# Query, key and value columns of the first attention layer as seven block products per group, in a stage of their own

## The chip, the cores and the metric

The kernel runs on one core of a Trainium2 chip. The metric is the device time of one execution in microseconds (us), the median of several executions. The core's engines are TensorE (PE in the profile, with its weight loads as PEld), VectorE (DVE), ScalarE (ACT), GpSimd (POOL) and SyncE (SP). SP and ACT also issue the DMAs: a row "SPq" or "ACTq" is such an issue.

## The reference

The reference is a trunk of two layers on 1024 tokens of width 1024. Each layer normalizes its input, multiplies it by one wide matrix, runs a token mixer and a cross attention into 256 memory tokens, multiplies by a gate and adds an output projection to the input. Only the first layer's mixer is of interest here:

```
cols = h @ w_in_a                                # 1024 tokens x 1024 -> 9216 columns for the mixer
qkv = cols.reshape(B, S, 3, N_GROUPS, A_HEADS, HEAD_DIM)
q = rms_norm(qkv[:, :, 0], q_gain); k = rms_norm(qkv[:, :, 1], k_gain); v = qkv[:, :, 2]
q = apply_partial_rotary(q, cos, sin); k = apply_partial_rotary(k, cos, sin)
for g, (window, dil) in enumerate(((128, 1), (512, 4), (2048, 16))):
    o, lse = dilated_window_attention(q[:, :, g], k[:, :, g], v[:, :, g], dil, window // dil)
alpha = softmax(stack(lses)); o = sum(alpha * outs)      # per head, over the three groups
```

So there are nine column blocks of 1024 x 1024 (query, key and value for three groups g = 0, 1, 2 with dilations 1, 4 and 16), each of eight heads of 128 columns. A query of a group sees at most 129 keys, its own and those before it at steps of the dilation.

## The kernel before

**Precision.** Each float32 operand of a projection is split in two, a rounded part and the remainder ("hi" and "lo"; for weights `wh` and `wl`), and three matmuls per 128 rows of depth (hi x hi, hi x lo, lo x hi) stand for one exact product. `piece` (L195 issues the load) brings a 128x1024 piece of weights from DRAM into `raw`; ACT rounds it to `wh` (L166, the line of the copy helper) and DVE forms `wl` (L212). `project` (L252 to L254) is the inner loop: a tile of 128 tokens stands still in PE, 512 weight columns stream past it, 24 matmuls for a tile and a block of 512 columns.

**Stages.** From 0 to about 70 us the input is normalized and transposed into `hhi` and `hlo`, and the first half of the gate's columns is projected. To about 245 us the memory's keys and values and the memory queries follow, with the cross attention and four slices of its gate (`gate_mem`). To 1250 us six rounds run, one for each half Q of the heads and each group g, from dilation 16 to dilation 1. A round projects keys, values and queries of four heads (`project_tiles`, eight token tiles each) and keeps keys and values in SBUF. After it come the second half of the gate and the output projection (to about 1420 us), then the second layer (to the end), which the change leaves alone.

**Within a round.** A key or query tile goes through `head_norm`: ACT squares it (`sq`, L300), DVE sums (L302), POOL raises to the power -1/2 (`rsqrt`, L175), DVE scales it out of PSUM (`qn`, L305). POOL then rotates it (`rotary`, L894 to L898), PE transposes four heads (`heads_T`, L311), and ACT copies them out (keys L1003, queries L166). As soon as a query tile is there, `attend` runs for the tile before it: scores (L954 to L957), mask and row maximum on DVE (L963), exponential on ACT (L965), transposes (L970), copy to SBUF on DVE (L972), values (L976). Its instructions stand among the next query tile's matmuls in PE's queue. Groups 1 and 2 write their outputs and row statistics to DRAM (`o_scr`, `st_scr`); group 0 reads them back and merges the three (`merge`; ACT scales one at L926, DVE adds the others at L929).

**Order of the tokens.** The token tiles are kept in the order by residue that the group in hand needs; before dilation 4 and before dilation 1 the whole operand is copied into another order (`second_order`, `first_order`).

**What sets the order.** Every engine works through its own queue in program order, with semaphores between the engines; a scheduler puts the emitted instructions in queue order, mostly as they are written. Weights are taken from a plan (`ahead`, `take`): loads go out on SP's queue some pieces ahead. ACT also issues all DMAs that write to DRAM, in line with its computing.

## Time and profile before

| | |
|---|---|
| median of 3 runs | 2154.14 us (2151.47 to 2155.81) |
| span of the profiled execution | 2151.6 us |
| PE busy | 2131.4 us, 99% |
| DVE, ACT, POOL busy | 1059.3, 730.2, 370.5 us |
| the six rounds | 245 to 1250 us |
| DMA traffic | 183.49 MB |

The profiled execution's own time is its span, 2.5 us under the median of the runs. The rows of the profile are shown in the prediction. A row of groups reads: line, engine, operation, output<-inputs, partitions x elements, count; then the time busy and the mean duration of one in ns; then the idle time of that engine just ahead of them, and what ended it.

### The profile page before, as it was taken

How to read it: one execution, taken by the hardware profiler on the slowest of the kernel's cores; microseconds unless marked ns; L12 is line 12 of the kernel's file. 1: busy time of each engine (PE TensorE's matmuls, PEld its weight loads, DVE VectorE, ACT ScalarE, POOL GpSimd, SP SyncE). 2: the span in 40 equal slices, each digit the busy share in tenths (PEclk: the TensorE clock that was granted, in tenths of full speed). 3: DMA queues.
4: the chain of work that ended last, by engine and by line, in shares of the span. 5: the costliest groups of instructions: out<-in, count | busy, mean ns of one | idle time of the engine just before them, and what ended most of it. 6: DMA issues, size and time to landing. Idle time of an engine off the chain costs nothing. (4 is left out here: it accounts for less than half of the span.)

```text
span 2151.6 us, 29608 instructions
## 1 busy us (share of the span) xinstructions
PE 2131.4 (99%) x11273; PEld 1812.9 (84%) x11273; DVE 1059.3 (49%) x2403; ACT 730.2 (34%) x1507; POOL 370.5 (17%) x600
## 2 busy tenths in 40 slices
PE   8999999999999999999999999999999999999999
PEld 6888888888888888888888978888888888888887
DVE  6755323424414314425834755434557772776443
ACT  4545323323423323323422532233532221232211
POOL 1013212312313302312222100012200000000221
PEclk9999999999999999999999999999999999999999
DMA  6543211221221121111411375431301112112633
GB/s 201 135 145 65 54 41 53 65 59 43 57 70 50 49 59 50 50 49 55 117 57 51 117 249 180 129 97 44 103 22 56 57 55 59 50 57 91 235 121 114
DMA packets 181004, 183.49 MB, mean 85 GB/s; under 512 B 49008, under 2 KB 117760, under 8 KB 180864
## 3 DMA queue, kind: packets, MB, share of 16 engines
q1 hardware_dynamic: 116592, 138.48, 21.1%
q10 hardware_dynamic: 64272, 43.13, 7.1%
q8 instruction: 89, 1.46, 0.3%
q14 instruction: 51, 0.42, 0.1%
HBM read 138.45 MB, written 43.12 MB: 84 GB/s over the span
## 5 line engine op out<-in xcount | busy, mean ns | idle before, releaser
L254 PE MATMUL acc<-wh,hlo 128*128 128x512 f32 x1440 | 565.3, 394 | 0.0
L253 PE MATMUL acc<-wl,hhi 128*128 128x512 f32 x1440 | 565.2, 393 | 0.0
L252 PE MATMUL acc<-wh,hhi 128*128 128x512 f32 x1440 | 563.1, 394 | 1.4 <-ACT wh L166 1.1
L175 POOL TENSOR_TENSOR rr<-rv,nhalf 128x4 f32<-128x4 f32 (+1 forms) x150 | 147.4, 983 | 1372.2 <-DVE rv L173 1346.5
L212 DVE TENSOR_TENSOR wl<-raw,wh 128x1024 fp32r<-128x1024 f32 x152 | 187.9, 1238 | 377.4 <-ACT wh L166 375.7
L252 PEld LDWEIGHTS acc<-wh,hhi 128*128 128x128 f32 x1440 | 271.1, 188 | 55.2 <-ACT wh L166 1.5
L253 PEld LDWEIGHTS acc<-wl,hhi 128*128 128x128 f32 x1440 | 270.9, 188 | 53.4 <-DVE wl L212 0.4
L254 PEld LDWEIGHTS acc<-wh,hlo 128*128 128x128 f32 x1440 | 270.7, 188 | 53.2
L166 ACT ACTIVATE wh<-raw 128x1024 fp32r<-128x1024 f32 x152 | 160.7, 1058 | 189.7 <-PE acc L254 55.2
L540 PE MATMUL acc<-hhi,wl 128*128 128x512 f32 x512 | 203.8, 398 | 0.0
L539 PE MATMUL acc<-hlo,wh 128*128 128x512 f32 x512 | 203.6, 398 | 0.0
L538 PE MATMUL acc<-hhi,wh 128*128 128x512 f32 x512 | 202.9, 396 | 0.0
L302 DVE TENSOR_REDUCE ss<-sq 128x4 f32<-128x512 f32 x116 | 79.2, 683 | 144.3 <-ACT sq L300 144.1
L635 PE MATMUL acc<-wh,yhi 128*128 128x512 f32 x360 | 143.2, 400 | 3.2 <-ACT yhi L166 3.2
L636 PE MATMUL acc<-wl,yhi 128*128 128x512 f32 x360 | 141.6, 393 | 0.0
L637 PE MATMUL acc<-wh,ylo 128*128 128x512 f32 x360 | 140.5, 395 | 0.0
L300 ACT ACTIVATE sq<-acc 128x512 f32<-128x512 f32 x116 | 68.9, 594 | 181.2 <-PE acc L254 177.1
L305 DVE TENSOR_TENSOR qn<-acc,rr 128x512 f32<-128x512 f32 x116 | 79.6, 688 | 93.5 <-PE pt L311 50.6
L965 ACT ACTIVATE pa<-pa,st 128x128 f32<-128x128 f32 (+1 forms) x192 | 84.4, 442 | 99.5 <-DVE st L963 95.4
L539 PEld LDWEIGHTS acc<-hlo,wh 128*128 128x128 f32 x512 | 96.3, 188 | 17.9
L538 PEld LDWEIGHTS acc<-hhi,wh 128*128 128x128 f32 x512 | 96.3, 188 | 17.6
L540 PEld LDWEIGHTS acc<-hhi,wl 128*128 128x128 f32 x512 | 96.3, 188 | 17.6
(241 smaller groups left out, 3193.3 us busy)
## 6 DMA issues: line engine op xcount, KB each, us to landing
raw<-in_w_in_a_dram SPq DMA_DIRECT2D x88, 512.0 KB
raw<-in_w_in_b_dram SPq DMA_DIRECT2D x40, 512.0 KB
o_scr<-os ACTq DMA_DIRECT2D x48, 256.0 KB
raw<-in_w_mem_kv_dram SPq DMA_DIRECT2D x16, 512.0 KB
os<-o_scr SPq DMA_DIRECT2D x32, 256.0 KB
raw<-in_w_out_a_dram SPq DMA_DIRECT2D x12, 512.0 KB
raw<-in_w_out_b_dram SPq DMA_DIRECT2D x12, 512.0 KB
gt<-gateb_scr SPq DMA_DIRECT2D x24, 256.0 KB
```

Source lines behind the costliest of these rows:

```text
L166: A.activation(dst, src, AF.Copy)
L175: G.tensor_tensor(r[:], v[:], nhalf[:, :n], op=OP.pow)
L212: rests.append(W_LO.tensor_tensor(lo[:], raw[:], hi[:].bitcast(F32), op=OP.subtract).ins)
L252: T.matmul(ps, hi, wh[:, j, :], start=at == 0, stop=False)
L253: T.matmul(ps, hi, wl[:, j, :], start=False, stop=False)
L254: T.matmul(ps, lo, wh[:, j, :], start=False, stop=at == n - 1)
L538: T.matmul(to, wh[:, k, :], mh, start=k == 0, stop=False)
L539: T.matmul(to, wh[:, k, :], ml, start=False, stop=False)
L540: T.matmul(to, wl[:, k, :], mh, start=False, stop=k == 7)
L635: T.matmul(pss[ch][:], hi[:, k, :], wh[:, j, :], start=first and k == 0, stop=False)
L636: T.matmul(pss[ch][:], hi[:, k, :], wl[:, j, :], start=False, stop=False)
L637: T.matmul(pss[ch][:], lo[:, k, :], wh[:, j, :], start=False, stop=end and k == 3)
```

## The change

For each of the nine column blocks, the matrix of 1024 tokens by 1024 rows of depth and the matrix of 1024 rows by 1024 columns are cut into four 512x512 blocks each. The ordinary product needs eight products of such blocks; the scheme of Strassen and Winograd needs seven, and sums of blocks ahead of and behind them.

- The tokens stay in natural order throughout. `x_pair` makes the operand two token tiles at a time (tile j and tile j+4) and with it the four sums s1 to s4 of input blocks, rounded on ACT, with remainders on POOL. s1 takes the place of a block (a21), which is kept in DRAM and read back during the last group.
- `load` brings the four weight blocks of a group from DRAM, `combine` forms their sums on POOL (eight passes of 128x1024 per group), `split_side` rounds them on ACT and forms the remainder on DVE, one product ahead.
- `product` runs a product: four token tiles of 12 matmuls. ACT copies the results of the first three products to SBUF; DVE adds later ones to these out of PSUM (four passes on POOL, L950 of the kernel after).
- `projected` does norm, rotary, transposes and the copy out, now from SBUF, and writes queries and keys to DRAM (`qk_scr`): one DMA per tile for group 0, four for groups 1 and 2, which put the tokens into residue order in runs of 32 tokens (128 bytes) or 16 tokens (64 bytes). Values go to `v_scr`.
- All nine groups are done first (keys, values, queries for g = 2, 1, 0), then the memory stage, then attention. Attention runs by pairs of heads: 12 pairs, eight tiles each, with queries, keys and values fetched two pairs ahead (`fetch`). Scores for two key blocks are one float32 product. The weighted sum of the groups is made by POOL (three passes for two tiles) and DVE (two).
- The memory gate's slices move: two stand in the memory stage, one is written ahead of attention, one between dilation 4 and dilation 1. The reordering copies and an extra pair of weight buffers go.

What stands in the queues now is shown at three places. First PE's queue at the first attention of dilation 16 (`s` scores, `pt` transposed probabilities, `po` output). Before it was:

```order
L254 MATMUL acc<-wh,hlo 128x512
L957 MATMUL s<-kT,qT 128x128
L970 MATMUL pt<-ident,pa 128x128 x2
L957 MATMUL s<-kT,qT 128x128
L970 MATMUL pt<-ident,pa 128x128 x2
L957 MATMUL s<-kT,qT 128x128 x2
L252 MATMUL acc<-wh,hhi 128x512
L253 MATMUL acc<-wl,hhi 128x512
L254 MATMUL acc<-wh,hlo 128x512
```

and after the change, behind the last product of the memory's cross attention (`po<-pml,vmh`):

```order
L398 MATMUL po<-pml,vmh_7779 128x256
L1078 MATMUL s<-kT,qT 128x128 x6
L1093 MATMUL pt<-ident,pa 128x128 x2
L1078 MATMUL s<-kT,qT 128x128 x2
L1093 MATMUL pt<-ident,pa 128x128 x2
L1078 MATMUL s<-kT,qT 128x128 x2
L1101 MATMUL acc<-vv,pts 128x128 x2
L1093 MATMUL pt<-ident,pa 128x128 x2
L1078 MATMUL s<-kT,qT 128x128 x2
```

The projection's matmuls that stood between the steps of attention are gone; the steps of two or three tiles alternate with one another.

Second ACT's queue where the keys of dilation 16 end and the values begin. Before, with `kT` the keys' place in SBUF and `vv` the values':

```order
L300 ACTIVATE sq<-acc 128x512 x2
L166 ACTIVATE wh<-raw 128x1024 x2
L1003 ACTIVATE kT<-pt,gqk 128x512 x2
L300 ACTIVATE sq<-acc 128x512
L166 ACTIVATE wh<-raw 128x1024 x2
L1003 ACTIVATE kT<-pt,gqk 128x512 x2
L166 ACTIVATE vv<-acc 128x512 x6
```

After, with `os` the transposed heads and `x_` the first results of the next group:

```order
L910 ACTIVATE os<-pt,gqk 128x4x16x8
L154 ACTIVATE x_1706<-acc 128x512
L918 DMA qk_scr_97<-os 128x8x16 x4
L910 ACTIVATE os<-pt,gqk 128x4x16x8
L154 ACTIVATE x_1735<-acc 128x512
L918 DMA qk_scr_97<-os 128x8x16 x4
L910 ACTIVATE os<-pt,gqk 128x4x16x8
L154 ACTIVATE x_1751<-acc 128x512
L154 ACTIVATE wh<-raw 128x1024
L918 DMA qk_scr_97<-os 128x8x16 x4
```

Each tile of keys now leaves four DMAs on ACT's queue, and the last tiles of a group stand among the next group's copies out of PSUM.

Third POOL's queue in the first key group, where `raw` is a weight block:

```order
L880 TENSOR_TENSOR c<-t_967,t_968 128x4x32
L950 TENSOR_TENSOR y_1040<-y_1040,x_786 128x512
L842 TENSOR_TENSOR raw<-raw 128x1024
L950 TENSOR_TENSOR y_1063<-y_1063,x_815 128x512
L950 TENSOR_TENSOR y_1079<-y_1079,x_831 128x512
L163 TENSOR_TENSOR rr_1007<-rv_1005,nhalf 128x4
L950 TENSOR_TENSOR y_1095<-y_1095,x_847 128x512
```

where POOL had in a round of keys:

```order
L175 TENSOR_TENSOR rr_2535<-rv_2533,nhalf 128x4
L894 TENSOR_TENSOR t_2539<-qn,rc 128x128
L896 TENSOR_TENSOR t_2540<-qn,rs 128x4x16 x2
L898 TENSOR_TENSOR qn<-t_2539,t_2540 128x4x32
L175 TENSOR_TENSOR rr_2557<-rv_2555,nhalf 128x4
```

The sums of weight blocks and of results now stand between the norm's and the rotary's steps.

The diff, cut to what the prediction speaks of:

```diff
-MGP = ((0,),(1,),(),())
-MG1 = (2, 3)
+MG0, MG1 = (0, 1), (2, 3)
...
+        groups = [(i, g) for g in (2, 1, 0) for i in (1, 2, 0)]
+        SIDE = ("a12", "a11", "s1", "s2", "s3", "a22", "s4")
...
+        def split_side(n, h):
+            src = raws[gi, FROM[p], h]
+            hi = wpool.tile([128, 1024], F32R, name="wh")
+            lo = wpool.tile([128, 1024], F32R, name="wl")
+            copy(W_HI, hi[:], src)
+            W_LO.tensor_tensor(lo[:], src, hi[:].bitcast(F32), op=OP.subtract)
+            split[n, h] = [t[:].rearrange("p (k n) -> p k n", k=2) for t in (hi, lo)]
+        def combine(gi, out, a, b, h):
+            G.tensor_tensor(raws[gi, out, h], raws[gi, a, h], raws[gi, b, h], op=OP.subtract)
...
+            if i == 0:
+                split_side(n + 1, 0)
+                split_side(n + 1, 1)
+            if p == 0 and i in (1, 2):
+                combine(gi, "12", "12", "11", i - 1)
+            if p == 1 and i in (1, 2):
+                combine(gi, "12", "22", "12", i - 1)
+            if p == 2 and i in (1, 2):
+                combine(gi, "11", "12", "11", i - 1)
+            if p == 3 and i in (1, 3):
+                combine(gi, "21'", "12", "21'", i // 2)
...
+        def projected(i, g, Q, m, c):
+            if i == 2:
+                SQ.dma_start(tile_of(v_scr[g], m)[:, Q * 512:(Q + 1) * 512], c.rearrange("p h d -> p (h d)"))
...
+            sq = pS.tile([128, 4, 128], F32, name="s")
+            A.activation(sq[:], c, AF.Square)
+            V.tensor_tensor(c, c, bc(r[:, :, None], [128, 4, 128]), op=OP.mult)
+            rotary(c, m)
+            t = heads_T(c)
+            o = gs.tile([128, 4, 128], F32, name="os")
...
+            A.activation(to, of, AF.Copy, scale=gqk[:, g:g + 1] if i else 1.0)
...
+            at = m % 4 * 32 if g == 1 else m * 16
+            view = scr.rearrange("p h (a r c) -> p h a r c", a=3 - g, r=n)[:, :, m // 4 if g == 1 else 0, :, at:at + RUN[g]]
+            for h in range(4):
+                SQ.dma_start(view[:, h], o[:, h].rearrange("p (r l) -> p r l", r=n))
...
+            for i in range(4):
+                ps = pp.tile([128, 4, 128], F32, name="acc")[:]
+                sides = [operand(SIDE[p], w)[:, :, i * 128:(i + 1) * 128] for w in ("hi", "lo")]
+                for kt in range(4):
+                    wh, wl = (t[:, kt % 2, :] for t in split[n, kt // 2])
+                    hi, lo = (s[:, kt, :] for s in sides)
+                    T.matmul(flat, hi, wh, start=kt == 0, stop=False)
+                    T.matmul(flat, hi, wl, start=False, stop=False)
+                    T.matmul(flat, lo, wh, start=False, stop=kt == 3)
+                if p == 0:
+                    xs[i] = room(f"x{i}")
+                    copy(A, xs[i], ps)
+                elif p == 1:
+                    c = room("c", bufs=3)
+                    V.tensor_tensor(c, xs[i], ps, op=OP.add)
+                    copy(A, xs[i], ps)
+                    projected(i_, g, 0, i, c)
+                elif p == 2:
+                    ys[i] = room(f"y{i}")
+                    copy(A, ys[i], ps)
+                elif p == 3:
+                    V.tensor_tensor(xs[i], xs[i], ps, op=OP.add)
+                    G.tensor_tensor(ys[i], ys[i], xs[i], op=OP.add)
+                elif p == 4:
+                    c = room("c", bufs=3)
+                    V.tensor_tensor(c, ys[i], ps, op=OP.add)
+                    V.tensor_tensor(xs[i], xs[i], ps, op=OP.add)
+                    projected(i_, g, 1, 4 + i, c)
+                elif p == 5:
+                    V.tensor_tensor(xs[i], xs[i], ps, op=OP.subtract)
+                    projected(i_, g, 0, 4 + i, xs[i])
+                else:
+                    V.tensor_tensor(ys[i], ys[i], ps, op=OP.add)
+                    projected(i_, g, 1, i, ys[i])
+                weights_ahead(n, i)
...
+        for j in range(4):
+            if j < 3:
+                x_pair(j + 1)
...
+            pss = [pp.tile([128, 512], F32, name="acc") for _ in range(2)]
+            project([ps[:] for ps in pss], [lhs_natural(j), lhs_natural(j + 4)], W,
...
+            keep_s1(j)
+        last = 7 * len(groups) - 1
+        for n in range(last + 1):
+            product(n, (lambda i, h: ahead(1 + h) if i == 3 else None) if n == last else None)
+            if n == last - 4:
+                for i, w in enumerate(("hi", "lo")):
+                    LQ.dma_start(operand("a21", w).bitcast(F32), a21_scr[i])
...
+            def fetch(at):
...
+                g, hp = heads[at]
+                q, k = (ap_.tile([128, 2, S], F32, name=n) for n in ("qT", "kT"))
+                for i, t in ((1, k), (0, q)):
+                    LQ.dma_start(t[:], qk_scr[i][g][:, 2 * hp:2 * hp + 2])
...
+            def scores(g, hp, m):
...
+                for hh in range(2):
+                    rhs = k[:, hh].rearrange("p (b k) -> p b k", k=128)[:, blocks[0]:m + 1:back]
+                    T.matmul(s[:, hh, :n].rearrange("p (b k) -> p b k", k=128), q[:, hh, m * 128:(m + 1) * 128], rhs, start=True, stop=True)
+                p = ap_.tile([128, 2, 256], F32, name="pa", bufs=3)
+                for hh in range(2):
+                    V.tensor_tensor_reduce(p[:, hh, :n], s[:, hh, :n], mk, scale=-SCALE, scalar=3.0e38,
+                                           op0=OP.add, op1=OP.min, accum_out=st[:, m, 0, hh:hh + 1])
+                    A.activation(p[:, hh, :n], p[:, hh, :n], AF.Exp, scale=-1.0, bias=st[:, m, 0, hh:hh + 1],
+                                 accum_out=st[:, m, 1, hh:hh + 1])
+                return p, blocks
...
+            def values(g, hp, m, p, blocks):
+                for hh in range(2):
+                    for i in range(nb):
+                        T.transpose(t[:, hh * nb + i, :], p[:, hh, i * 128:(i + 1) * 128], ident[:])
+                pts = ap_.tile([128, 4, 128], F32, name="pts")
+                V.tensor_copy(pts[:, :2 * nb, :], t[:, :2 * nb, :])
...
+                for hh in range(2):
+                    for i, b in enumerate(blocks):
+                        T.matmul(o[:, m % 2 * 2 + hh, :], pts[:, hh * nb + i, :], v[:, b, hh * 128:hh * 128 + 128],
+                                 start=i == 0, stop=i == nb - 1)
...
+            def merge(hp, m, o, st):
+                og = others(hp, m)
...
                 for g in (1, 2):
-                    for h in range(4):
-                        V.scalar_tensor_tensor(y[:, h, :], o[g - 1][:, h, :], w[:, g, h:h + 1], y[:, h, :],
-                                               op0=OP.mult, op1=OP.add)
+                    G.tensor_tensor(og[g - 1], og[g - 1], wg(g), op=OP.mult)
+                G.tensor_tensor(og[0], og[0], og[1], op=OP.add)
+                y = ap_.tile([128, 4, 128], F32, name="os")
+                V.tensor_tensor(y[:], o[:], wg(0), op=OP.mult)
+                V.tensor_tensor(y[:], y[:], og[0], op=OP.add)
...
-            for Q, g in group_order:
-                if (Q, g) == (0, 1):
-                    t = kpool.tile([128, NT, 4, 128], F32R, name="kl")[:].rearrange("p (k m) h t -> p k (m h t)", k=4)
-                    second_order({(n, k): t[:, 2 * i + k, :] for i, n in enumerate(("hi", "lo")) for k in range(2)})
-                elif (Q, g) == (0, 0):
-                    first_order()
...
-                def each_k(m, ps):
-                    n = head_norm(ps, ap_)
-                    rotary(n, g, 1, m)
-                    t = heads_T(n)
-                    A.activation(kT[:, m], t[:], AF.Copy, scale=gqk[:, g:g + 1])
...
-                def each_q(m, ps):
-                    n = head_norm(ps, ap_)
-                    rotary(n, g, 0, m)
-                    t = heads_T(n)
-                    q = at_.tile([128, 4, 128], F32 if g else F32R, name="qT")
-                    if g:
-                        copy(A, q[:], t[:])
...
+            fetch(0)
+            gate_mem(MG1[0])
+            fetch(1)
+            waiting = []
+            for at, (g, hp) in enumerate(heads):
+                if at and at + 1 < len(heads):
+                    fetch(at + 1)
+                for m in range(NT):
+                    new = (g, hp, m, *scores(g, hp, m))
-                        attend(Q, g, *waiting.pop(), kT, kl, vv)
-                    waiting.append((m, q, ql.get(m), fetch_stats(Q, m) if g == 0 else None))
-                project_tiles(("k", Q, g), lhs, each_k, order)
...
-                project_tiles(("v", Q, g), lhs, each_v, order, end)
-                waiting = []
...
-                project_tiles(("q", Q, g), lhs, each_q, order, end)
-                last = lambda: attend(Q, g, *waiting.pop(), kT, kl, vv)
...
+                        values(*waiting.pop())
+                    waiting.append(new)
+                if (g, hp) == (1, 3):
+                    gate_mem(MG1[1])
...
+            gate_chunk(1, lambda: values(*waiting.pop()), leave, (ap_, "os"), to_out)
```

599 lines of the change are left out of this document (313 added, 286 removed).

## The prediction

> **What bounds the kernel now.** I read the page first: busy shares, the 40 slices, the chain of work that ended last.
>
> ```profile
> span 2151.6 us, 29608 instructions
> PE 2131.4 (99%) x11273; PEld 1812.9 (84%) x11273; DVE 1059.3 (49%) x2403; ACT 730.2 (34%) x1507; POOL 370.5 (17%) x600
> ...
> PE   8999999999999999999999999999999999999999
> ...
> PE 40%; DMA 1%; DVE 1%; issue 0%; ACT 0%; SPq 0%; POOL 0%; ACTq 0%; DVEq 0%
> ```
>
> TensorE (PE) is busy 99% of the span, nothing else above 49%, and what the chain attributes is nearly all PE. So the kernel is as long as PE's list of instructions. Then the table by stretches of time (columns: stretch, length, busy PE, PEld, DVE, ACT, POOL with counts, granted clock, DMA share, GB/s), and PE's own timeline:
>
> ```profile
> 70.00:245.00 175.00, 174.94 (x921) 149.00 (x920) 100.24 (x204) 87.40 (x182) 29.68 (x28) 1.00 0.44 110
> 245.00:1250.00 1005.00, 1004.05 (x5289) 856.56 (x5288) 414.46 (x1119) 350.99 (x822) 248.62 (x480) 1.00 0.22 62
> 450.00:500.00 50.00, 50.00 (x222) 41.41 (x221) 8.67 (x12) 9.51 (x13) 5.59 (x11) 1.00 0.14 42
> ```
> ```profile
> 560.81 0.39 PE L252 MATMUL acc<-wh,hhi 128*128 128x512 f32 x1
> ...
> 561.51 0.39 PE L252 MATMUL acc<-wh,hhi 128*128 128x512 f32 x1
> ...
> 562.20 0.39 PE L252 MATMUL acc<-wh,hhi 128*128 128x512 f32 x1
> ```
>
> The projections of query, key and value with their attention fill 245 to 1250 us without a hole, at full clock. A matmul lasts 0.39 us, but they overlap: three start in 0.70 us, and 222 fill a stretch of 50 us, 0.225 each. I take 0.227 us per 128x512 matmul. PE counts, so removing matmuls shortens the span, as long as the other engines keep PE fed.
>
> **What is removed.** Before: 18 weight blocks x 8 token tiles x 24 matmuls = 3456. After: 9 groups x 7 products x 4 tiles x 12 = 3024. 432 x 0.227 = **-98 us**. The head transposes (96 tiles of four) and the attention's products stay. What remains of 1005 us beside 3456 x 0.227 = 785 us is 220 us, and this is what it holds:
>
> ```profile
> L976 PE MATMUL po<-vv,pts 128*128 128x128 f32 x560 | 76.3, 274 | 0.0
> ...
> L970 PE MATMUL pt<-ident,pa 128*128 128x128 f32 x280 | 49.2, 272 | 0.5 <-ACT qT L166 0.5
> ...
> L957 PE MATMUL s<-kT,qT 128*128 128x128 f32 x320 | 45.2, 275 | 0.0
> ```
> ```profile
> 1045.72 1.05 PE L976 MATMUL po<-vv,pts 128*128 128x128 f32 x8
> ```
>
> Eight records take 1.05 us, the last one's 0.27 of latency included: 0.11 each, and a product of float32 has two records, a transpose one. The three rows with the first group's scores are then 155 us, the 384 head transposes 42. The other 23 us are switches between projection and attention; after the change neither is threaded through the other, and I take half of it back: **-12 us**.
>
> **What the other engines must do beside the products.** Per query or key group PE needs 28 tiles x 12 x 0.227 + 64 transposes x 0.11 = 83 us (a value group 76). The rows:
>
> ```profile
> L212 DVE TENSOR_TENSOR wl<-raw,wh 128x1024 fp32r<-128x1024 f32 x152 | 187.9, 1238 | 377.4 <-ACT wh L166 375.7
> L166 ACT ACTIVATE wh<-raw 128x1024 fp32r<-128x1024 f32 x152 | 160.7, 1058 | 189.7 <-PE acc L254 55.2 <-PE acc L539 48.5 <-DMA raw<-in_w_in_a_dram 36.5
> L175 POOL TENSOR_TENSOR rr<-rv,nhalf 128x4 f32<-128x4 f32 x132 | 137.1, 1039 | 1117.5 <-DVE rv L173 1091.8 <-DVE mw L918 20.1 <-DVE mmx L397 5.4
> L305 DVE TENSOR_TENSOR qn<-acc,rr 128x512 f32<-128x512 f32 x116 | 79.6, 688 | 93.5 <-PE pt L311 50.6 <-POOL rr L175 41.3 <-PE pt L970 1.3
> L302 DVE TENSOR_REDUCE ss<-sq 128x4 f32<-128x512 f32 x116 | 79.2, 683 | 144.3 <-ACT sq L300 144.1
> L300 ACT ACTIVATE sq<-acc 128x512 f32<-128x512 f32 x116 | 68.9, 594 | 181.2 <-PE acc L254 177.1 <-DVE ss L302 3.2 <-DVE rv L173 0.7
> L896 POOL TENSOR_TENSOR t<-qn,rs 128x64 f32<-128x64 f32 x192 | 63.6, 352 | 0.0
> ...
> L898 POOL TENSOR_TENSOR qn<-t,t 128x128 f32<-128x128 f32 x96 | 47.9, 499 | 6.0
> L894 POOL TENSOR_TENSOR t<-qn,rc 128x128 f32<-128x128 f32 x96 | 44.8, 467 | 166.8 <-DVE qn L305 128.8 <-DVE rv L173 31.5 <-PE s L957 3.2
> ...
> L1352 POOL TENSOR_TENSOR ylo<-y,yhi 128x512 fp32r<-128x512 f32 x24 | 32.4, 1354 | 103.8 <-ACT yhi L166 103.8
> ...
> L1003 ACT ACTIVATE kT<-pt,gqk 128x512 f32<-128x512 f32 x32 | 22.0, 687 | 39.0 <-PE pt L311 38.8
> ...
> L403 POOL TENSOR_TENSOR pm<-pm,mden 128x512 f32<-128x512 f32 x16 | 16.7, 1041 | 47.8 <-DVE mden L402 26.1 <-DVE mmx L397 21.1 <-DVE rv L173 0.6
> ```
>
> DVE: 14 weight remainders x 1.24, 16 reductions x 0.68, 16 scalings and 24 sums of products x 0.69 = 56 us: it fits. POOL: per tile 1.04 + 0.47 + 2 x 0.35 + 0.50 = 2.71, x 16 = 43 us; the four adds of L950 at 1.3 are 5; the eight weight combinations of 128x1024 don't occur before: twice the 512-wide rows is 2.1 to 2.7 us, I take 2.5, by the wider of the two: 20. Together 69 of 83 us. Twelve of the sixteen tiles come in the last three products, so POOL runs late into the next group, whose first combinations queue behind it. I put **+15 us** (0 to 60) on this: each of six groups may make PE wait for a weight by up to 10 us, and what a value group follows is caught up.
>
> The bound is soft because POOL and DVE disturb each other (POOL's rows, then DVE's):
>
> ```profile
> 434.90 0.46 POOL L894 TENSOR_TENSOR t<-qn,rc 128x128 f32<-128x128 f32 x1 [1.75 <-DVE qn L305]
> 435.32 1.58 POOL L896 TENSOR_TENSOR t<-qn,rs 128x64 f32<-128x64 f32 x2
> ```
> ```profile
> 435.14 1.30 DVE L212 TENSOR_TENSOR wl<-raw,wh 128x1024 fp32r<-128x1024 f32 x1 [0.32 <-ACT wh L166]
> ```
>
> Two rotary steps that need 0.35 each took 1.58 us beside a weight remainder. [...]
>
> ACT, in the groups of dilation 16: 14 x 1.06 + 12 copies of results at 0.6 + 16 squares x 0.59 + 16 evacuations x 0.69 = 43 us, and 64 DMA issues. The nearest issues are of 1024 runs of 128 bytes:
>
> ```profile
> 227.54 1.25 ACTq L424 DMA_DIRECT2D om_scr<-os  x2
> ```
> ```profile
> q10 hardware_dynamic: 23040, 2.91, 26.7%
> ```
>
> Two take 1.25 us, and ACT does nothing else meanwhile; four in a row are some 2.6, so 16 x 2.6 = 42 us, and ACT has 85 us to do in 83. Dilation 4 issues half as many runs, and dilation 1 one DMA per tile: they fit. Behind these issues on ACT stand the copies that empty PSUM for the next group. A backlog is worked off in the value group, which asks ACT for under 30 of 76 us: **+12 us** (0 to 30). The packets: 23040 in 70 us (175 to 245, queue 10) took 26.7% of 16 engines, 13 ns each; a tile's 4096 are then 3.3 us, 53 per group, hidden.
>
> **Attention by itself.** Before, attention lay between the matmuls of the query projections, which covered every wait. Now PE has only attention to do there, and the slowest engine of each unit (two heads, one tile) counts:
>
> ```profile
> L965 ACT ACTIVATE pa<-pa,st 128x256 f32<-128x256 f32 x88 | 43.8, 500 | 40.6 <-DVE st L963 36.5 <-DMA o_scr<-os 4.1
> ...
> L965 ACT ACTIVATE pa<-pa,st 128x128 f32<-128x128 f32 x104 | 40.6, 393 | 58.9 <-DVE st L963 58.9
> L929 DVE SCALAR_TENSOR_TENSOR os<-os,mw 128x128 f32<-128x128 f32 x128 | 39.9, 358 | 8.7 <-ACT os L926 8.7
> ...
> L965 ACT ACTIVATION_READ_ACCUMULATOR pa<-pa,st 128x1 f32 x192 | 36.1, 188 | 0.0
> ...
> L963 DVE CUSTOM_DVE_ANT_0 pa<-s,masks 128x256 f32<-128x256 f32 x88 | 33.3, 418 | 0.6
> ...
> L972 DVE COPY pts<-pt 128x512 f32<-128x512 f32 x44 | 30.0, 686 | 31.9 <-PE pt L970 31.9
> ...
> L963 DVE DVE_READ_ACCUMULATOR2_ANT st<- 128x1 f32 x192 | 15.9, 83 | 0.0
> ```
>
> Dilation 16: PE 10 records x 0.11 = 1.1 us; ACT 2 x (0.39 + 0.19) and half an evacuation of 0.59 = 1.5; 32 units: 50 against 35. Dilation 4: half of its units have two key blocks (PE 20 records, 2.2; ACT 2 x (0.50 + 0.19) + 0.3 and more for DMA issues): 57 against 53. Dilation 1: DVE 2 x (0.42 + 0.08) + 0.69, and for the merge two 512-wide passes per pair of units (0.69 each; before four of 0.36 per group) with small ones, 2.5 per unit: 82 against 66. Sum 189 for 155: **+34 us** (5 to 60).
>
> **Seams.** The order shows that the first attention loads wait for the last memory attention; the first head pair's query, key and value are 3 MB, at 249 GB/s (the best slice below) 12 us, of which some 8 are bare. Memory attention's last units lack projection beside them (four half units of about 2): 8. Entry to the products, and from there to the memory stage: 4 each, for some four instructions in a chain, of 0.6 to 1.2 us each. **+24 us** (12 to 40).
>
> ```profile
> GB/s 201 135 145 65 54 41 53 65 59 43 57 70 50 49 59 50 50 49 55 117 57 51 117 249 180 129 97 44 103 22 56 57 55 59 50 57 91 235 121 114
> ```
>
> **Edits at nothing.** The first stage (70 us before) gets sums of input blocks, four DVE passes of 0.69, four ACT copies and four POOL passes of 1.3 per pair of token tiles: some 5 us of POOL beside 24 x 2 x 0.227 = 11 us of gate products, one pair ahead. The four memory gate slices stand elsewhere with the same matmuls; one now lies between dilation 4 and 1, and its weight load (512 KB) passes SP's queue among the fetches: 2 us at the rate below. Dropping the two reorderings of the operands saves DVE and ACT passes that lay beside PE's work. Query, key and value go out and in again once: 36 MB in, 36 out, of which the writes lie in the product stage, whose DMA share is 0.22, and the reads in attention: 4 MB per head pair with what is spilled, 16 us at most, beside some 12 to 20 us of work. Without that cover dilation 16 alone would lose 4 x 4 us, which is in the upper end of the attention term.
>
> **Sum** on the profiled execution: 2151.6 - 98 - 12 + 15 + 12 + 34 + 24 = 2126.6. The profiled span is 2.5 us under the median of the runs shown (2154.1); so I forecast **2129 us**, 25 faster.
>
> **Rivals.**
> 1. *Nearly all is hidden.* POOL and ACT add nothing, attention costs 16 (its third group only, where DVE has the most), the seams 16: 2154 - 98 - 12 + 32 = 2076. For it: DVE at 56 and POOL at 69 of 83 us, on paper. Against: the bursts in the last three products.
> 2. *POOL becomes the bound of the six query and key groups; slower.* If POOL's work and DVE's passes with two SBUF inputs (14 remainders at 1.24, 16 scalings at 0.6 to 0.69, now from SBUF: 27 us) never overlap, 69 + 27 = 96 us stand against 83 to 84: 12 x 6 = 73 in place of my 15: 2129 + 58 = 2187. It decides from POOL plus those passes above 83 us a group. For it: the 1.58 row; against: POOL's power steps are 17 of the 69 us and mostly overhead.
> 3. *The scatter is the bound; slower.* If a 64-byte run costs 27 ns rather than 13, about twice the small packets above, a tile takes 6.9 us and a group 110, +27 twice: 2129 + 54 = 2183. Against: the packet row.
> 4. *The change doesn't cut PE's work,* because more small steps eat the 432 matmuls. The counted list excludes it.
>
> **Chances.** Forecast 0.46 (its own range 2105 to 2150), rival 1 0.20, rival 2 0.22, rival 3 0.08, 2 and 3 together 0.04. The range takes in most of rival 1 and reaches past rivals 2 and 3: 2068 to 2200. A measurement here tells 0.2% (4 us) from no change. Faster: 0.42 of the forecast, all of rival 1, 0.02 = 0.64; the same: 0.03 + 0.02 = 0.05; slower: 0.31.
>
> **What would show it.** Product groups of 83 us in the table by stretches mean the first term holds; 95 and waits of PE for weights that wait for POOL mean rival 2; waits behind the scatter's DMA issues or for its buffer mean the ACT term or rival 3; an attention stage of about 190 us with DVE or ACT as releaser confirms the fourth term. A cadence above 0.23 us in the products, or a clock below 1.00 in the attention stage, would make the prediction wrong in a place that I don't price.

## The result and the profile after

The changed kernel takes 2193.23 us (median of 4 runs, 2188.43 to 2194.40) where the kernel before takes 2153.76 (median of 4 runs, 2151.47 to 2155.81). The ratio is 1.0175, with an interval of 1.0161 to 1.019: slower by 1.75%. The time lies inside the stated range, but on the other side of no change than the forecast.

The page of the kernel after (busy time and share of each engine with the number of instructions, PE and its clock in 40 slices, the chain that ended last):

```profile
span 2192.5 us, 29737 instructions
...
PE 2093.1 (95%) x10713; PEld 1744.3 (80%) x10713; DVE 1300.3 (59%) x2524; ACT 827.6 (38%) x1567; POOL 745.5 (34%) x772
...
PE   7999998999999999897889899999999999999999
...
PEclk9999999999999999999899999999999999999999
...
PE 44%; DMA 3%; DVE 2%; ACT 1%; issue 0%; ACTq 0%; POOL 0%; SPq 0%; DVEq 0%
```

PE has 560 instructions fewer, and its busy time fell by 2131.4 - 2093.1 = 38 us, much less than the 98 us of the matmuls removed. Its idle time rose from 20 to 99 us. POOL's busy time doubled. So PE was no longer fed without a break, and part of what it still did had become slower.

The stages of the kernel after (columns as in the prediction: stretch, length, busy PE, PEld, DVE, ACT, POOL with counts, granted clock, DMA share, GB/s). They are the first stage, the nine groups of products, the memory stage, attention, and the rest:

```profile
0.00:73.80 73.80, 58.11 (x257) 45.02 (x258) 58.02 (x100) 45.79 (x77) 26.15 (x26) 0.98 0.52 163
73.80:853.50 779.70, 749.20 (x3388) 605.90 (x3387) 503.99 (x644) 325.49 (x422) 536.68 (x573) 0.99 0.47 112
853.50:1041.70 188.20, 169.47 (x872) 140.48 (x870) 95.13 (x179) 86.04 (x180) 40.78 (x49) 0.96 0.40 121
1041.70:1274.30 232.60, 203.05 (x1342) 180.77 (x1343) 147.66 (x612) 113.54 (x438) 55.55 (x48) 0.95 0.76 252
1274.30:2192.40 918.10, 913.29 (x4860) 772.10 (x4859) 495.49 (x991) 256.70 (x452) 86.31 (x78) 1.00 0.31 100
```

The same view of the kernel before, for the two stretches that the prediction doesn't show:

```profile
0.00:70.00 70.00, 59.97 (x284) 49.02 (x285) 51.38 (x96) 34.74 (x57) 6.05 (x14) 1.00 0.56 181
...
1250.00:2151.60 901.60, 892.41 (x4783) 758.28 (x4782) 493.17 (x986) 257.08 (x448) 86.16 (x78) 1.00 0.31 99
```

Each stage can be set against the other kernel's, with matmuls that moved from one to another counted at 0.227 us and transposes at 0.11. Attention is the simplest: of its 232.6 us, 72 gate matmuls are 16 us and a memory gate slice of 48 matmuls is 11; 205.6 remain, where before had 155. The nine groups should take 3024 x 0.227 + 364 x 0.11 = 726.5 us, and took 779.7. The memory stage before was 175 us less 51 matmuls of the rounds (11.6) that already stood in it; 30 slice matmuls fewer and 28 transposes more make it 159.7, and it took 188.2. In the same way the first stage has 64.8 (70 less 19 slice matmuls and 8 transposes) to compare with its 73.8, and the rest 921.6 (901.6 and 84 gate matmuls and 8 transposes) with 918.1.

| us | forecast | measured |
|---|---|---|
| 432 matmuls removed | -98 | -98 |
| "switches" between projection and attention | -12 | 0 |
| first stage, entry to the products | +4 | +9 |
| products, beyond their matmuls and transposes | +15 +12 | +53 |
| memory stage: tail, entry, first fetch | +20 | +29 |
| attention | +34 | +51 |
| the rest | 0 | -3 |
| sum | -25 | +41 |

The right column closes on the two spans: 2192.5 - 2151.6 = 40.9. So no single stage is to blame; four of them each cost more than they were given, and one gain was not there. Each row comes from one profiled execution: in four kernels whose edits leave the products alone (e4, e6, e7, e10) that stage took 785.9 to 787.2 us, where this page has 780, so a row is good to some 6 us.

The three kinds of product groups (keys and values of dilation 16, keys of dilation 4):

```profile
73.80:161.80 88.00, 83.15 (x370) 67.15 (x369) 68.20 (x80) 38.73 (x52) 68.47 (x65) 0.98 0.55 126
161.80:247.60 85.80, 81.92 (x370) 65.87 (x369) 43.55 (x54) 30.58 (x36) 46.62 (x45) 1.00 0.59 135
...
332.40:427.70 95.30, 87.07 (x397) 69.60 (x396) 67.95 (x93) 46.99 (x60) 77.03 (x90) 0.98 0.53 100
```

A first reading would take the 95 us for the second rival, POOL as the bound. But POOL is busy 68 to 77 of 88 to 95 us, about as forecast (69), and PE is busy 83 to 87 where its matmuls and transposes need 83 at full speed. Who makes PE wait in the nine groups is in the list of waits (total, times, longest):

```profile
PE pt L298 <- POOL c L880: 13.2, 13, 2.5
PE acc L932 <- ACT x L154: 11.2, 6, 2.9
```

The first row is a transpose of heads that waits for the end of POOL's rotary (with the same wait for other tiles 17 us in all), the second the first matmul of a tile that waits until ACT has emptied a PSUM bank. No row shows a wait for a weight that waits for POOL. Together that is half of the 53 us. The rest must lie in what PE is busy with, and two things were found there.

The first is the clock. Two stretches one behind the other, same columns, the clock third from the end; and PE's timeline across their border (start, duration, then in brackets the wait ahead):

```profile
357.20:360.60 3.40, 1.20 (x6) 0.66 (x4) 2.77 (x3) 1.06 (x2) 2.24 (x2) 1.00 0.76 78
360.60:364.00 3.40, 2.94 (x7) 2.36 (x8) 2.00 (x2) 1.93 (x4) 3.40 (x3) 0.50 0.66 75
```
```profile
358.01 0.39 PE L934 MATMUL acc<-wh,hlo 128*128 128x512 f32 x1
361.06 0.80 PE L932 MATMUL acc<-wh,hhi 128*128 128x512 f32 x1 [2.66 <-ACT x L154]
361.65 0.63 PE L933 MATMUL acc<-wl,hhi 128*128 128x512 f32 x1
362.08 0.63 PE L934 MATMUL acc<-wh,hlo 128*128 128x512 f32 x1
362.51 0.63 PE L932 MATMUL acc<-wh,hhi 128*128 128x512 f32 x1
```

PE waits 2.66 us, and behind that wait the granted clock is 0.50 for 3.4 us: matmuls start 0.43 us apart rather than 0.23. So this wait of 2.66 us costs some 1.5 us more, half of the 2.94 us that PE works in the second stretch. The mean granted clock over the span is 0.988; half speed for x us gives 0.5x = 0.012 x 2192.5, so x is about 53 us, in twelve places. The kernel before has one such stretch of 3.4 us (mean clock 0.999), behind a wait of 2.65 us at 1261.5. Where PE works in them, half the time is lost: some 22 us in all, an estimate from PE's busy time of about 45 us there.

The length of a wait alone doesn't decide. Nine of the twelve places lie behind a single wait of 2.3 us or more, three behind shorter ones (2.05 us; 0.96 and 0.97; 0.43 and 0.69). And behind a wait of 2.50 us at 195.0 us the clock stays at 1.00:

```profile
193.34:196.75 3.41, 1.67 (x8) 1.05 (x6) 0.69 (x1) 2.71 (x3) 2.79 (x2) 1.00 0.96 145
196.75:200.16 3.41, 2.65 (x12) 2.20 (x13) 1.68 (x2) 1.80 (x4) 0.00 (x0) 1.00 0.99 167
```

In the clock records of this trace the twelve stretches last 3.413 us, or two or three times that, and they begin whole multiples of 3.413 us apart, from 46.58 to 1231.01 us, to within 0.004 us. So the granted clock changed here on a fixed grid of windows. The two rows are windows of that grid, and the wait is divided between them. In the traces of the kernel before and the kernel after, from 17 us on, 10 windows at full clock had PE busy for less than 1.45 us, and half clock followed all of them; 1215 had it busy for more than 2.25 us, and half clock followed none; of the 16 between, 3. The window ahead of the stretch at 360.6 us was not idle: PE was busy for 1.20 of its 3.40 us.

The second is the place of an operand, which experiments e1, e5 and e9 settle below.

### The profile page after: what moved, and what is told of

The parts are those of the page before. It is cut to its first block, busy times and chain, and to the rows that moved or that the text cites. A ratio compares the mean times of both kernels' runs of the same rounds, so it can differ in the third digit from the quotient of the medians.

```text
span 2192.5 us, 29737 instructions
## 1 busy us (share of the span) xinstructions
PE 2093.1 (95%) x10713; PEld 1744.3 (80%) x10713; DVE 1300.3 (59%) x2524; ACT 827.6 (38%) x1567; POOL 745.5 (34%) x772
## 4 chain that ended last, share of the span: by engine, by line
PE 44%; DMA 3%; DVE 2%; ACT 1%; issue 0%; ACTq 0%; POOL 0%; SPq 0%; DVEq 0%
PE acc L475 5%; PE acc L474 5%; PE acc L476 5%; PE acc L562 4%; PE acc L563 4%; PE acc L564 4%; PE acc L240 3%; PE acc L238 3%; PE acc L239 3%; DMA o_scr<-os 2%; PE pt L1282 1%; PE s L1282 1%; PE s L1078 1%; PE po L1416 1%; PE pt L281 1%; PE s L1385 1%
## 5 line engine op out<-in xcount | busy, mean ns | idle before, releaser
L163 POOL TENSOR_TENSOR rr<-rv,nhalf 128x4 f32<-128x4 f32 (+1 forms) x150 | 162.4, 1088 | 782.3 <-DVE rv L161 765.4
L154 ACT ACTIVATE wh<-raw 128x1024 fp32r<-128x1024 f32 x206 | 215.6, 1056 | 256.6 <-PE acc L934 123.6
L838 DVE TENSOR_TENSOR wl<-raw,wh 128x1024 fp32r<-128x1024 f32 x126 | 189.3, 1509 | 109.0 <-ACT wh L154 108.7
L932 PE MATMUL acc<-wh,hhi 128*128 128x512 f32 x576 | 229.4, 398 | 11.8 <-ACT x L154 11.2
L842 POOL TENSOR_TENSOR raw<-raw 128x1024 f32<-128x1024 f32 x72 | 176.5, 2470 | 170.3 <-DVE wl L838 133.9
L933 PE MATMUL acc<-wl,hhi 128*128 128x512 f32 x576 | 227.7, 395 | 0.0
L934 PE MATMUL acc<-wh,hlo 128*128 128x512 f32 x576 | 227.5, 395 | 0.0
L200 DVE TENSOR_TENSOR wl<-raw,wh 128x1024 fp32r<-128x1024 f32 x80 | 98.5, 1234 | 121.2 <-ACT wh L154 120.6
L240 PE MATMUL acc<-wh,hlo 128*128 128x512 f32 x384 | 151.6, 396 | 5.8 <-DVE hlo L259 5.8
L238 PE MATMUL acc<-wh,hhi 128*128 128x512 f32 x384 | 150.8, 397 | 0.8 <-ACT wh L154 0.8
L239 PE MATMUL acc<-wl,hhi 128*128 128x512 f32 x384 | 151.3, 394 | 0.0
L932 PEld LDWEIGHTS acc<-wh,hhi 128*128 128x128 f32 x576 | 109.4, 190 | 37.2 <-ACT x L154 13.7
L934 PEld LDWEIGHTS acc<-wh,hlo 128*128 128x128 f32 x576 | 109.3, 190 | 22.4
L933 PEld LDWEIGHTS acc<-wl,hhi 128*128 128x128 f32 x576 | 109.4, 190 | 22.1 <-DVE wl L838 0.3
```

The costliest lines, as they stand in the source:

```text
L238: T.matmul(ps, hi, wh[:, j, :], start=at == 0, stop=False)
L239: T.matmul(ps, hi, wl[:, j, :], start=False, stop=False)
L240: T.matmul(ps, lo, wh[:, j, :], start=False, stop=at == n - 1)
L932: T.matmul(flat, hi, wh, start=kt == 0, stop=False)
L933: T.matmul(flat, hi, wl, start=False, stop=False)
L934: T.matmul(flat, lo, wh, start=False, stop=kt == 3)
```

## The experiments

All times are medians, and a gain is the difference to the 2193.2 us of the kernel after (ratio 1.0175 to the kernel before, interval 1.0161 to 1.019). Each run's ratio is to runs of the kernel before on its own chip.

**e3: the scattered writes go out on SP's queue.** ACT's timeline in the kernel after, at the start of the keys of dilation 4, while the last queries of dilation 16 are still being written (ACTq rows are DMA issues):

```profile
356.75 2.55 ACTq L918 DMA_DIRECT2D qk_scr<-os  x4
359.54 1.04 ACT L910 ACTIVATE os<-pt 128x512 f32<-128x512 f32 x1 [2.82 <-DMA qk_scr<-os]
360.39 0.62 ACT L154 ACTIVATE x<-acc 128x512 f32<-128x512 f32 x1
```

Four issues take 2.55 us of the 2.82 in which ACT computes nothing, then it reorders the heads (1.04), and only then empties the PSUM bank for which PE had been waiting since 358.4.

```diff
-                SQ.dma_start(view[:, h], o[:, h].rearrange("p (r l) -> p r l", r=n))
+                LQ.dma_start(view[:, h], o[:, h].rearrange("p (r l) -> p r l", r=n))
```

> The four DMAs per tile of dilations 16 and 4 are issued on SP's queue in place of ACT's; packets and places are the same. Theory ACT's queue (the ACT term of the prediction): PE's waits for the copies that empty PSUM at the four group changes, 11 us with three stretches of half clock behind them, go: 11 to 17 us less, 2179. Theory packets (rival 3): the transfers set the pace wherever they are issued: within 3 us. Theory SP: weight loads stand behind the issues and come late: PE waits for weights, and it is slower.

2179.3 us, ratio 1.0113 (1.0098 to 1.0128): 13.9 us gained. PE's waits in the products:

```profile
PE pt L298 <- POOL c L880: 10.7, 9, 3.0
PE acc L932 <- ACT x L154: 2.5, 3, 1.6
```

The waits for ACT fall from 11.2 to 2.5 us, and the half clock behind them goes too. ACT's part in the write to DRAM is therefore real and has the forecast's size (+12). It's the issues in ACT's queue, not the packets, which are the same in e3: in the stretch from 340 to 362 us of the kernel after, queue 10 moves

```profile
q10 hardware_dynamic: 25259, 1.59, 65.0%
```

packets, MB and share of 16 engines: 22 us x 16 x 0.65 / 25259 = 9.1 ns for a packet of 64 bytes, a third of what rival 3 needed.

**e2: weight blocks are combined on DVE, not on POOL.** POOL's timeline in the first group of the kernel after:

```profile
106.43 2.03 POOL L878 TENSOR_TENSOR t<-c,rs 128x64 f32<-128x64 f32 x2
108.42 2.36 POOL L842 TENSOR_TENSOR raw<-raw 128x1024 f32<-128x1024 f32 x1
110.75 1.43 POOL L880 TENSOR_TENSOR c<-t,t 128x128 f32<-128x128 f32 x1
```

A combination stands between two steps of one rotary, and the three together take 5.8 us; PE waits for the last of them from 109.7 to 112.2.

```diff
-            G.tensor_tensor(raws[gi, out, h], raws[gi, a, h], raws[gi, b, h], op=OP.subtract)
+            V.tensor_tensor(raws[gi, out, h], raws[gi, a, h], raws[gi, b, h], op=OP.subtract)
```

> The eight combinations of weight blocks per group on DVE in place of POOL (the result is the same). Theory POOL (rival 2, in its mild form): PE's waits for POOL's rotary in the product stage, 17 us in the changed kernel, fall under 5, and the half-clock stretch after the longest of them goes: 15 to 20 us less, 2175. Rival 2 in its full form would give 50 or more. Theory DVE (its queue takes the place): DVE gets 10 us more per group, 66 to 76 of 83 to 95 us, and the waits move there: no gain, or up to 10 us more.

2184.58 us, ratio 1.0136 (1.0116 to 1.0156): 8.7 us gained. The list of waits of this kernel:

```profile
PE acc L932 <- ACT x L154: 21.1, 6, 7.0
PE pt L298 <- POOL c L880: 4.2, 4, 1.8
```

Waits for POOL's rotary fall from 13.2 to 4.2 us, but waits for ACT's copies rise from 11.2 to 21.1: what came late by POOL now comes late by ACT. The products are no shorter for it. These are the products and the memory stage of e2:

```profile
73.00:856.30 783.30, 751.24 (x3389) 608.80 (x3389) 522.60 (x714) 325.21 (x421) 363.21 (x499) 0.98 0.47 111
856.30:1036.80 180.50, 165.59 (x871) 137.04 (x869) 96.34 (x180) 85.99 (x180) 42.90 (x51) 0.99 0.40 127
```

The products take 783 us where the kernel after has 780. What is gained lies mostly in the memory stage, 180.5 us for 188.2: a wait of 4.8 us at its entry (for ACT's rounding of the memory tokens) is gone, and so is the half clock behind it. The two bottlenecks lie one behind the other, and in the products this edit alone gains nothing.

**e1, e5, e9: the place of the operands in SBUF.** In the kernel after, products with the input blocks themselves run at 0.227 us per matmul, those with the sums s2, s3, s4 at 0.232 to 0.235, as do the output projections. The blocks start at a multiple of 256 bytes of a partition, the sums 32 bytes behind one (places come from the kernel's layout; a trace doesn't show them); the output projections' operands, too, have moved from a multiple of 256 to 32 behind one. A small tile that nothing uses lies ahead of them and is made longer, by 32, 96 and 224 bytes:

```diff
-    small.tile([128, 40], F32, name="left", bufs=1)
+    small.tile([128, 48], F32, name="left", bufs=1)
```

with 64 in place of 48 for e5, and 96 for e9.

> The changed kernel with 32 bytes of padding ahead of everything that lies behind the small tiles in SBUF; nothing else. In its trace the products with s2, s3 and s4 as the stationary side start a matmul every 233 ns, those with a block of the input every 227; the sums' tiles begin 32 bytes off a multiple of 64, the input's on one, and so does the output projections' yhi (233 and 235 ns). Theory address: 1296 matmuls of the sums and 1152 of the output projections go to 227 ns: 15 to 17 us less, 2177. Theory rival 2 (POOL or DVE in the way in the last products): the cadence of the sums' products stays at 233, and the time within 3 us of 2193.

> As e1_align, with 96 bytes of padding, so that the sums and yhi begin on a multiple of 128 bytes, as the input's blocks do in both kernels and yhi does before the change (e1 put them 64 off it, and their matmuls stayed at 233 ns). Theory address: 233 to 227 ns in the products of s2, s3 and s4 and in both output projections, 2448 matmuls by 6 ns, 15 us less: 2178. If the cadence stays, the cause is another than the place (the sums' shape, or what runs beside them): 2193.

> As e1 and e5, with 224 bytes of padding, so that the sums and yhi begin on a multiple of 256 bytes, as the input's blocks do (17152 is 67 times 256) and as yhi did before the change; at 32, 64 and 128 off such a multiple their matmuls stayed at 232 to 233 ns. Theory address: 227 ns in the products of s2, s3 and s4 and in both output projections, 2448 matmuls by 6 ns: 13 to 15 us less, 2179. If the cadence stays at 232, place in this sense isn't the cause.

e1 (the sums at 64 behind a multiple of 256): 2193.13 us, ratio 1.0175 (1.016 to 1.019), nothing gained, the cadence (from one matmul's start to the next) still 0.233. e5 (at 128): 2188.65 us, ratio 1.0179 (1.0143 to 1.0214), the cadence 0.232. Both were misses: it wasn't the multiple of 64 or of 128. e9 (at 256): 2181.5 us, ratio 1.012 (1.0104 to 1.0135), 11.7 us gained, and all products and output projections at 0.227. The same product in PE's timeline, the kernel after and e9:

```profile
655.18 0.40 PE L932 MATMUL acc<-wh,s3hi 128*128 128x512 f32 x1
...
656.58 0.40 PE L932 MATMUL acc<-wh,s3hi 128*128 128x512 f32 x1
```
```profile
653.13 0.39 PE L932 MATMUL acc<-wh,s3hi 128*128 128x512 f32 x1
...
654.49 0.39 PE L932 MATMUL acc<-wh,s3hi 128*128 128x512 f32 x1
```

Six matmuls take 1.40 us in the one and 1.36 in the other. With 1295 matmuls of sums in the products at 6 ns and 1080 in the output projections (three lines of 360) that is 14 us, near to the 11.7 measured. A term that I had looked for only as a "cadence above 0.23 us" is worth as much as the scatter.

**e12: work in place of waiting.** If waits cause the half clock, PE should keep its clock when it has something to do in them. Twenty-two transposes of the identity into PSUM that nothing reads are put ahead of each of four tiles whose first matmul waits; the three half-clock stretches behind these waits in the kernel after, from 360.6, 463.0 and 623.4 us, should then be gone:

```diff
+                if (gi, p, i) in ((1, 2, 2), (3, 1, 3), (4, 2, 2), (6, 1, 3)):
+                    with tc.issue_after(lastmm[0]):
+                        fill(22)
```

> The changed kernel with 22 transposes of the identity (2.4 us of PE, into a PSUM tile that nothing reads) ahead of each of the four tiles at which PE waits 2.3 to 2.9 us for ACT's copies (group 1, third product; group 3, second; group 4, third; group 6, second). They add nothing to the result and lie inside the waits. [...]

2189.44 us, ratio 1.0167 (1.0153 to 1.0181): 3.8 us gained. The table by stretches of e12:

```profile
357.00:366.00 9.00, 7.57 (x45) 6.42 (x44) 4.55 (x6) 4.13 (x6) 7.84 (x4) 1.00 0.66 73
459.00:468.00 9.00, 9.00 (x53) 7.77 (x52) 2.36 (x2) 4.65 (x7) 2.36 (x2) 1.00 0.42 109
620.00:629.00 9.00, 9.00 (x53) 7.79 (x52) 8.07 (x9) 4.88 (x8) 7.84 (x5) 1.00 0.36 58
```

The clock is 1.00 in the three, where the kernel after has 0.81 in the same stretches. With the count by windows above, this shows that the half clock in these three places followed from PE's idleness. What a stretch costs, the time doesn't show: by PE's busy time the three are worth about 1.6 us each (half of 2.94 to 3.40), 5 us together, an estimate. The 3.8 us are not clear of noise (the intervals of the two ratios overlap), and in e12's trace the products take 781.0 us, no less than before.

**e7: without most of attention's fetches.** Attention by stretches in the kernel after, dilations 16, 4 and 1 (the third with the gate slice and gate matmuls, 27 us), and the chief waits in it:

```profile
1041.70:1094.10 52.40, 42.37 (x292) 39.01 (x293) 26.67 (x153) 31.26 (x133) 0.00 (x0) 0.85 0.89 325
1094.10:1165.20 71.10, 58.24 (x406) 51.45 (x405) 36.01 (x164) 39.74 (x149) 0.00 (x0) 0.98 0.79 257
1165.20:1274.30 109.10, 102.44 (x648) 90.30 (x647) 84.98 (x296) 42.54 (x158) 55.55 (x48) 0.98 0.69 214
```
```profile
PE po L1101 <- ACT os L154: 12.6, 6, 5.1
PE s L1078 <- DMA qT<-qk_scr: 9.6, 2, 9.2
...
ACT os L154 <- DMA o_scr<-os: 26.2, 11, 5.2
```

PE waits for ACT's copy of an output, and ACT itself (last row) waits for a buffer whose write to DRAM hasn't landed. In e7 the pairs after the first two take the queries, keys and values of those two; their own fetch is left out.

```diff
+                if at < 2:
...
+                else:
+                    q, k, v, _ = held[heads[at - 2]]
```

> Leaves out the fetch of queries, keys and values for all but the first two head pairs; later pairs compute on these. 30 of 36 MB of reads go from the attention stage, and everything else stays. Theory DMA (the fetches make the writes of the outputs slow, and the stage waits for both): the stage, 233 us from the first scores to the last values, falls by 25 to 40. Theory chain (DVE and ACT by unit, 189 us, and the seams' half clock are what is left): by under 12 us.

2164.58 us, ratio 1.0043 (1.0027 to 1.006): 28.6 us less. Its three dilations:

```profile
1046.30:1083.70 37.40, 36.95 (x299) 35.66 (x300) 26.29 (x154) 31.76 (x135) 0.00 (x0) 0.94 0.62 219
1083.70:1134.50 50.80, 50.80 (x400) 49.10 (x398) 36.03 (x164) 39.01 (x149) 0.00 (x0) 1.00 0.33 102
1134.50:1247.10 112.60, 104.36 (x649) 91.32 (x647) 87.24 (x296) 42.08 (x156) 55.10 (x48) 0.97 0.43 123
```

Dilation 16 falls from 52 to 37 us and dilation 4 from 71 to 51, PE busy for all of it; dilation 1 doesn't gain. So DMA traffic sets the first two dilations, and the third doesn't depend on it. Four pairs of dilation 16 at 3 MB of reads and 1 MB of writes (4.2 million bytes) are 16.8 MB, and 325 GB/s over 52.4 us are 17.0: the stage moves little else. This agrees, but it is no second proof, since the rate is read from the same stretch.

**e4: four output buffers rather than two.**

```diff
-                os = ap_.tile([128, 4, 128], F32, name="os")
+                os = ap_.tile([128, 4, 128], F32, name="oo", bufs=4)
```

> Four buffers in place of two for the attention stage's outputs on their way to DRAM. Theory latency of the spill (an output waits for the write of the one before the last, 5 to 9 us each beside the fetches): PE's 12.6 us of waits for these copies and ACT's 26 go, with the half-clock stretches behind the longest: 12 to 20 us less, 2177. Theory DMA bandwidth (16 engines at 79% over the whole stage are the limit of dilation 16): the waits move to the fetches, under 5 us.

2186.86 us, ratio 1.0132 (1.0109 to 1.0156): 6.4 us gained. The waits for that copy fall from 12.6 to 2.9 us, those for other steps of attention grow by about 6, and the stage goes from 232.6 to 224.2 us in the trace (227 to 233 in e1, e2, e3, e5, e9 and e12, whose edits leave it alone). The interval of the ratio lies just below that of the kernel after.

**e6 and e10: the first fetch earlier.** Both were to remove the bare 9.2 us ahead of the first scores. e6 laid attention's buffers out anew in their pool; e10 gives queries, keys and masks a pool of their own on the other side of SBUF, opened when the products end.

```diff
+        aq = sr.enter_context(tc.tile_pool(name="attq", bufs=2, side="right"))
...
-                q, k = (ap_.tile([128, 2, S], F32, name=n) for n in ("qT", "kT"))
+                q, k = (aq.tile([128, 2, S], F32, name=n) for n in ("qT", "kT"))
```

> The attention stage's buffers are laid out so that the first queries, keys and masks lie in SBUF that the memory attention doesn't use; nothing else. Theory seam: PE's 9.2 us of wait for the first queries goes, and most of the 10 us of half clock around it (1020 to 1031 us): 12 to 15 us less, 2179. Theory latency (the same wait turns up at the first values, whose buffer keeps its place, or the fetch runs early anyway): under 4 us.

> Masks, queries and keys of the attention stage in a pool of their own that opens ahead of the memory stage, so that the first pairs are fetched during it (in e6 the buffers had moved, but the loads kept the wait for the last memory attention). Theory seam: PE's 9 us of wait for the first queries and the half clock around it go: 12 to 15 us less, 2179; with the second pair there too, dilation 16 (52 us) gets up to 8 us shorter. Theory e6 (the seam's wait passes on to the first values): under 4 us.

e6: 2199.33 us, ratio 1.0205 (1.019 to 1.0221). The loads still stand behind the last memory attention, so the run says nothing of an earlier fetch. e10: 2189.54 us, ratio 1.0165 (1.015 to 1.0181), 3.7 us gained, which is not clear of noise. The 9.2 us are gone, but a wait of 3.2 us for the values takes their place and dilation 16 grows from 52 to 58 us: its length is traffic, and the stage gained little from a start that wasn't earlier for all of it.

**e8 and e11: edits together.** e8 has e2, e3, e4, e5 and e6; e11 has e2, e3, e4, e9 and e10.

> The changed kernel with e2, e3, e4, e5 and e6 together. If the terms are separate they add: 9 and 14 and 6 measured, e2's the larger as the scatter no longer makes ACT late (12 to 20), and 15 and 13 expected: 2130 to 2145, faster than before (2154). If they share one hidden limit (PE's waits move on to the next one), 2155 to 2170.

> e2, e3, e4, e9 and e10 together: e8_all (2149.7) with the padding and the fetches mended. Theory separate terms: 12 to 15 us for the cadence and 12 to 20 for the seam off it: 2115 to 2125, faster than before by 1.4 to 1.8%. If the padding does nothing: 2130 to 2138.

e8: 2149.68 us, ratio 0.9974 (0.9963 to 0.9984). e11: 2141.63 us (5 runs), ratio 0.9935 (0.9922 to 0.9947), faster than both kernels, by 0.65% than the kernel before. The five gains of e11 taken one by one sum to 44 us, together they are 51.6. In the products POOL's and ACT's edits need each other: e3 alone has 769 us there, e2 alone 783, and e8, which has both, 758. The time of e11 is still above the 2115 to 2125 expected. Its products, memory stage and attention:

```profile
72.70:824.10 751.40, 734.32 (x3389) 601.56 (x3389) 522.38 (x714) 325.57 (x421) 366.44 (x499) 1.00 0.49 116
824.10:992.80 168.70, 162.59 (x840) 133.87 (x838) 93.76 (x173) 82.79 (x170) 40.87 (x49) 0.99 0.44 143
992.80:1226.40 233.60, 203.49 (x1376) 180.83 (x1375) 152.36 (x620) 116.72 (x448) 57.95 (x50) 0.97 0.76 246
```

The products are 25 us above the 726.5 that their matmuls and transposes need (53 in the kernel after), and PE still waits 14 us there for the rotary, though POOL combines no weights any more; the memory stage is shorter by 19.5, and attention is as long as it was, 246 GB/s all through. Most of what is left to gain lies there.

## Why the prediction went wrong

**The matmuls removed, -98: right.** The product stage has the 3024 matmuls counted, and where the operands lie well they run at 0.227 us. So rival 4 is excluded, and with the rest of the table rival 1: little was hidden.

**"The other 23 us are switches between projection and attention", half of which I took back: wrong.** The stretch from 245 to 1250 us of the kernel before holds 1184 records of L252, where the rounds have 1152; 17 of the rounds' stand ahead of 245, so 49 of each of three lines belong to the gate: 147 matmuls come in, 51 went out, net 96 x 0.227 = 22 us. There was no cost of switching, and nothing to win: a remainder was given a name without a look at what instructions stood in it. That is 12 us of the error.

**POOL, +15: near in size, wrong in kind.** PE waits 17 us for it, but not for weights, as I put it: it waits for the rotary. The weight combinations of 2.47 us that stand in it are only part of the cause. Without them e2 gains nothing in the products, e8 is 12 us below e3 there (769 and 758), and e11 keeps 14 us of these waits; what the rest comes from was not tried. POOL and DVE do slow each other; by groups of the kernel after:

```profile
L838 DVE TENSOR_TENSOR wl<-raw,wh 128x1024 fp32r<-128x1024 f32 x126 | 189.3, 1509 | 109.0 <-ACT wh L154 108.7
```

The same pass took 1238 ns before, and in e2, where POOL combines no weights, it takes 1252; a combination takes 1.23 us on DVE there. In the kernel after, 32 of the 126 passes have no POOL work beside them and take 1222 ns. POOL's step of 128x64 (L878) takes 323 ns with no DVE work beside it and 550 with some, the means of 46 and 146. That POOL's work and such passes never overlap, as rival 2 supposed, no run shows. Rival 2, POOL as the bound, came near the right time (2187) by luck: POOL has 12 to 26 us free in each query and key group.

**ACT and the scatter, +12: right.** The four issues take 2.55 us (2.6 forecast), and e3 gains 13.9, the half clock behind its waits included. Rival 3 is excluded by 9.1 ns per packet.

**Attention, +34: 17 too low, and for dilations 16 and 4 by the wrong engine.** Dilation 1 was forecast at 82 us, bound by DVE: 109.1 less 27 for gate work is 82, and e7 doesn't shorten it. Dilation 16 came to 52 (50 forecast), but by luck: ACT is busy for 31 of it, and without the fetches it takes 37. Dilation 4 came to 71 (57 forecast), and takes 51 without them. I had worked out the traffic, 4 MB and "16 us at most, beside some 12 to 20 us of work", and put it at nothing in the sum and into the upper end of the range. That is the step that failed: here the transfer, as long as the work, wasn't hidden. In e7 the stage is 201 us, 174 without the gate's 27, which is less than the 189 forecast, so all that it took above the forecast hangs on the fetches.

**Seams, +24 with the entry to the products: some 38 (9 in the first stage, 29 in the memory stage).** The bare first fetch is 9.2 us (8 forecast). Of the 14 us above the forecast half clock explains some 6, an estimate: half of PE's 3.4 us busy at half clock in the first stage and of 8.9 in the memory stage. The entry to the memory stage, forecast at 4, has a wait of 4.8 us and 2.8 of that half clock behind it, and e2 is without both. How the rest divides was not tried.

**What I didn't price.** The last sentence of the prediction names both: "A cadence above 0.23 us in the products, or a clock below 1.00 in the attention stage". The first is e9's 11.7 us; the second some 22 us in all stages (an estimate from PE's busy time; no run measures it), nearly all of which is counted in the table in the products, the memory stage and attention. In the products, waits of 30 us, half clock of 6.5 (half of PE's 13 us in four such stretches) and 8 for the sums' place make 45 of 53 us; 8 stay open.

Forecast and measurement are 66 us apart: 12 for the switches, 26 in the products, 17 in attention and 14 at the seams, less 3 in the rest. No single step turned the direction. Two causes run through several of them, some 22 us of half clock and 11.7 for the operands' place; even without both the change would have been some 7 us slower. PE waited for only 20 us in the kernel before, and its trace has a single half-clock stretch (from 1265.5 us, behind a wait of 2.65); I didn't look at it, and priced each new wait at its length.

## What to carry to other kernels

A change that takes work from an engine that never waits has to be priced by every place where the engine will wait: here nine of the eleven waits of 2.3 us or more in the kernel after were followed by 3.4 us or more at half clock, which by PE's busy time adds some 1.5 us (an estimate) for every 3.4. When intermediate results go through DRAM, set the bytes of each stage over the rate that the trace shows beside the stage's work, and expect the stage to take at least the longer of the two. Count the instructions in a stretch by kind before a remainder is explained, and compare the SBUF places of stationary operands before and after: 224 bytes of padding were worth 11.7 us here.
